# A second feed-forward net in two phases: gates and ups kept on chip, then the down product by seven block products

## The chip, the cores and the metric

The kernel runs on one core of a Trainium2 chip. Its engines run side by side, each through its own list of instructions in order: TensorE (PE; its weight loads are listed as PEld), VectorE (DVE), ScalarE (ACT), GpSimd (POOL) and SyncE (SP), which issues most transfers between the chip's main memory and the on-chip memory. Matmul results go to a second on-chip memory of eight banks, called PSUM in the code, from which VectorE and ScalarE read them. The metric is the time of one execution in microseconds of device time. Runs are repeated, and one execution is profiled.

## The reference, cut to what matters

Two layers of a diffusion backbone over 512 latent tokens and 256 context tokens, each with 1024 features. Layer 0 mixes tokens by gated linear attention and softmax attention, layer 1 by a gated recurrence; after each mixer stands a SwiGLU feed-forward net with a sandwich of norms and gates around it:

```python
def _swiglu(h, w_gate, w_up, w_down):
    return (jax.nn.silu(h @ w_gate) * (h @ w_up)) @ w_down
...
        x_lat = x_lat + m_lat[5] * _rms(_swiglu(h_lat, ffn_w_gate[l], ffn_w_up[l], ffn_w_down[l]), norm_post_ffn[l])
```

The hidden width is 2816, or 22 chunks of 128. In layer 1 only the 512 latent tokens go through the net. Everything is float32.

## The kernel before, in words

**Numbers.** Each float32 operand x of a large product is split into a high part H (a cast to the rounded format fp32r, on ScalarE) and a low part L = x - H (on VectorE). A product is then three matmuls, H H, H L and L H (`mm3`, line 679). Weights come in units of 128 x 1024 elements, 512 KB: one load into a `raw` tile (three buffers), one cast to `wH`, one subtraction to `wL` (four buffers each; `unit`, line 664).

**Gates and ups.** `h @ w_gate` and `h @ w_up` for a pair of chunks are made from block products after Strassen and Winograd: tokens, features and chunks are halved, and seven products of blocks take the place of eight (`SEVEN`, `seven`, line 768). `pair_operands` (line 730) loads two raw tiles and forms the sums of weight blocks on VectorE (line 752), which are split like the rest. A product of four feature blocks, three matmuls each, runs over n tokens; n is 256 in layer 1, 384 in layer 0. So a pair of chunks is 84 matmuls per weight. The banks are emptied by ScalarE and VectorE (lines 791 to 809) into a tile `go` for gates or `uo` for ups, one buffer each. The activation is applied in place at line 1572, the multiplication of ups by gates at line 1523.

**The loop of `ffn`** (line 1504) runs over the eleven pairs. The first pair, `first()`, is a plain product, begun while the norm before it still finishes. Then each turn makes a gate product, the part of the down product for the pair before (`acc_part`, line 811: 48 matmuls of 512 columns in layer 1, added to the result `y` by VectorE at line 820), and an up product. The gated pair is split at lines 1525 and 1526 into operands `gH` and `gL`, for which layer 1 reserves two sets (`forms.gated`). The last turn has no down part between; two down parts are then made together, and `post_norm` (line 644) closes each token tile: sum of squares, multiplication by the gate row, a power on GpSimd (line 600), and the last sum (line 659), which is stored.

**Order.** A scheduler behind the tile framework lays out each engine's list, by the order of the program and by readiness. Matmuls are pinned to program order only where `self.pinned` is set, which `ffn` does not do. Buffers of one tag are handed on when their readers are done; a pool opened where another was released waits for that pool's tiles one by one.

```python
        def gu(x):
            return fp.tile([P, 2, 2 * n], F32, tag=x, bufs=1, name=x)
...
            if c0 + 2 < NFC:
                if y is None:
                    y = yp.tile([P, len(tiles), D], F32, tag="y", bufs=1, name=f"y{l}")
                self.acc_part([(units(c0 - 2), cur)], n, tiles, singles, y, c0 == 2, fill)
                u = product(wu, c0, "uo")
```

Of the kernel before, what the change touches and what calls it, by code (L numbers as in the profile page):

```python
# [316 lines left out]
class Net:  # L317
# [29 lines left out]
    def mm(self, *a, **k):  # L347
        return self.pin(self.nc.tensor.matmul(*a, **k))  # L348
# [330 lines left out]
    def mm3(self, out, stat, mov, first, last):  # L679

        mm = self.mm
        mm(out, stat[0], mov[0], start=first, stop=False)
        mm(out, stat[0], mov[1], start=False, stop=False)
        mm(out, stat[1], mov[0], start=False, stop=last)

    def gemm_T(self, pt, W, h, groups, o=0):

# [77 lines left out]
            "U2": quarter(c, 0), "S4": quarter(c, 1), "V": quarter(d, 0),  # L765
        }

    def seven(self, W, h, X, fill, then=None):

        nc, n = self.nc, h.n  # L770
        ab = self.mm_tile("ab")
        bank = {"A": ab[:, :n], "B": ab[:, 512 : 512 + n]}
        c11, c12, c21, c22 = (X[:, i, n * k : n * k + n] for i in range(2) for k in range(2))
        for wn, hn, x in SEVEN:
            new = wn in ("11", "U1", "12", "22")
            if x not in bank:
                bank[x] = self.sc_tile(x, "ED".index(x))[:, :n]
# [12 lines left out]
            if wn == "11":  # L790
                nc.scalar.copy(c11, pt)  # L791
            elif wn == "U1":
                copy = nc.scalar.copy(c22, pt)
                if then is not None:
                    with self.tc.issue_after(copy.ins):
                        then()
                fill()
            elif wn == "12":
                nc.vector.tensor_tensor(c11, c11, pt, op=ALU.add)
            elif wn == "U2":  # L800
                nc.scalar.copy(c12, pt)
            elif wn == "22":
                nc.scalar.mul(c21, pt, -1.0)
                fill()
            elif wn == "S4":
                nc.vector.tensor_tensor(c12, c12, pt, op=ALU.add)  # L806
            else:
                nc.vector.tensor_tensor(c21, c21, pt, op=ALU.subtract)  # L808
                nc.vector.scalar_tensor_tensor(c22, pt, -1.0, c22, op0=ALU.mult, op1=ALU.subtract)  # L809
# [694 lines left out]
    def ffn(self, l, xp, yp, fp, pp, rp, h, ending, extra=None):  # L1504
# [95 lines left out]
        next(follow, None)  # L1600
        if gp is rp:
            rp.release()
        return y

    def run(self):
# [204 lines left out]

        def ending(ys):
            ep = self.open_pool("e1b")
            end = ender(ep, 1, 5, lat, xat(x1), lambda t: out[0, t * P : (t + 1) * P, :], None)

            def close():
                yield
                yield
                yield
                yield
                ep.release()  # L1820

            return end, close(), ep

        self.ffn(1, ha, yp, fp, pp, rp, forms, ending)
        fp.release()
        yp.release()
        ha.release()
        pad.release()


# [47 lines left out]
```

## Time and profile before

| what | value |
|---|---|
| runs, median of 3 | 1744.47 us (1738.44 to 1744.97) |
| profiled execution, its own time | 1732.31 us |
| span of the profiled execution, first to last instruction | 1730.5 us |
| mean granted TensorE clock | 0.999 |
| gates, ups and down product of layer 1, from the end of the first pair to the last matmul | 1391.7 to 1722.85 us |
| transfers, mean over the span | 108 GB/s |

A row of a group view names the line, the engine, the operation, the tile written and the tiles read, the shape and the count; then the busy time in microseconds, the mean of one in nanoseconds, and after the second bar the idle time of the engine just before these instructions, with what ended most of it. A row of the chain of waits gives a start, a length and the instructions that the end of the program goes back to. A row of windows gives a stretch of time and the busy microseconds of each engine in it, with the granted clock, the busy share of the transfer engines and their GB/s. A row of a timeline gives start, length, engine and instruction. A row of transfers gives the tile, the queue, the count, the size and the time from issue to landing. A row of waits gives who waited for whom: the sum in microseconds, the count, and the longest.

### The profile page before, as it was taken

To read this page: it belongs to the slowest core of one execution; us is meant where nothing else is said; L and a number is where in the kernel's file an instruction comes from. 1 tells how busy PE (TensorE), PEld (TensorE's weight loads), DVE (VectorE), ACT (ScalarE), POOL (GpSimd) and SP (SyncE) were. 2 spreads that over 40 slices of the span, in tenths; PEclk is the share of its full clock that TensorE was granted. 3 is DMA by queue.
4 is the path that set the end of the run, shared out by engine and by line. 5 is a ranking of instruction groups with operands and counts; after the bars stand their busy time and mean duration, and the time that the engine had idled before them with its cause. 6 is when DMAs were issued, how large, how long until landed. Compare 5 with 4: busy or idle time off the path is not lost. (4 is left out here: it accounts for less than half of the span.)

```text
span 1730.5 us, 32414 instructions
## 1 busy us (share of the span) xinstructions
PE 1681.9 (97%) x13512; PEld 1506.6 (87%) x13512; DVE 1288.3 (74%) x2061; ACT 863.7 (50%) x1496; POOL 73.3 (4%) x93
## 2 busy tenths in 40 slices
PE   7999998999999999999999999999999999999998
PEld 5899987888998889898997888889888899999997
DVE  5889668836969999796668328787864678878785
ACT  4745568746442323233346436666644754444342
POOL 1004110000000000000001000000000000000000
PEclk9999999999999999999999999999999999999999
DMA  9641012144334465452225222121114333333333
GB/s 321 195 143 39 2 62 88 61 134 146 111 97 144 133 193 171 131 179 62 74 86 186 82 73 62 42 59 51 50 62 141 116 110 99 94 102 110 94 102 122
DMA packets 169838, 187.22 MB, mean 108 GB/s; under 512 B 6454, under 2 KB 141148, under 8 KB 169692
## 3 DMA queue, kind: packets, MB, share of 16 engines
q1 hardware_dynamic: 167760, 181.56, 33.1%
q10 hardware_dynamic: 1932, 3.59, 0.6%
q8 instruction: 106, 1.74, 0.4%
q14 instruction: 40, 0.33, 0.1%
HBM read 175.66 MB, written 9.46 MB: 107 GB/s over the span
## 5 line engine op out<-in xcount | busy, mean ns | idle before, releaser
L348 PE MATMUL nat<-wH,x 128*128 128x256 f32 (+2 forms) x944 | 216.2, 319 | 5.1 <-ACT x L641 2.6
L673 DVE TENSOR_TENSOR wL<-raw,wH 128x1024 fp32r<-128x1024 f32 (+1 forms) x126 | 151.0, 1207 | 91.8 <-ACT wH L672 91.3
L727 ACT CAST wH<-raw 128x1024 fp32r<-128x1024 f32 x120 | 124.6, 1052 | 175.7 <-PE acc L348 73.6
L728 DVE TENSOR_TENSOR wL<-raw,wH 128x1024 fp32r<-128x1024 f32 x120 | 145.3, 1221 | 62.3 <-ACT wH L727 62.2
L348 PEld LDWEIGHTS nat<-wH,x 128*128 128x128 f32 x944 | 157.6, 190 | 21.5 <-ACT x L641 3.6
L348 PE MATMUL acc<-wH,gH 128*128 128x512 f32 x440 | 172.6, 393 | 0.0
L672 ACT CAST wH<-raw 128x1024 fp32r<-128x1024 f32 (+1 forms) x126 | 129.0, 1040 | 85.9 <-PE nat L348 25.2
L348 PE MATMUL acc<-wH,gL 128*128 128x512 f32 x440 | 171.7, 390 | 0.0
L348 PE MATMUL acc<-wL,gH 128*128 128x512 f32 x440 | 171.6, 390 | 0.0
L348 PE MATMUL nat<-wL,x 128*128 128x256 f32 (+2 forms) x472 | 148.6, 315 | 0.0
L820 DVE TENSOR_TENSOR y<-y,acc 128x1024 f32<-128x1024 f32 x135 | 114.9, 863 | 32.2 <-PE acc L348 28.8
L348 PE MATMUL ff<-x,wH 128*128 128x512 f32 (+1 forms) x512 | 127.5, 340 | 0.0
L530 DVE SCALAR_TENSOR_TENSOR macc<-mraw,scT,macc 128x1024 f32<-128x1024 f32 x98 | 123.0, 1281 | 5.0 <-DMA mraw<-in_mod_w_dram 4.7
L600 POOL TENSOR_TENSOR rs<-ms,neghalf 128x1 f32<-128x1 f32 (+2 forms) x62 | 57.2, 924 | 1582.6 <-DVE ms L598 1582.5
L348 PE MATMUL oproj<-wH,x 128*128 128x512 f32 x320 | 101.6, 395 | 0.0
L348 PEld LDWEIGHTS acc<-wH,gH 128*128 128x128 f32 x440 | 82.6, 188 | 19.7 <-issue 1.7
L348 PEld LDWEIGHTS acc<-wH,gL 128*128 128x128 f32 x440 | 82.6, 188 | 17.3
L348 PEld LDWEIGHTS acc<-wL,gH 128*128 128x128 f32 x440 | 82.7, 188 | 16.1
L348 PEld LDWEIGHTS ff<-x,wH 128*128 128x128 f32 x512 | 87.4, 190 | 10.0
L348 PEld LDWEIGHTS nat<-wL,x 128*128 128x128 f32 x472 | 89.8, 190 | 5.1
L923 ACT COPY qkh<-arr 128x512 f32<-128x512 f32 x112 | 70.1, 642 | 36.3 <-DVE arr L928 32.1
L348 PE MATMUL ff<-x,wL 128*128 128x256 f32 (+1 forms) x256 | 86.1, 337 | 0.0
(344 smaller groups left out, 4045.5 us busy)
## 6 DMA issues: line engine op xcount, KB each, us to landing
mraw<-in_mod_w_dram SPq DMA_DIRECT2D x80, 512.0 KB, 3.8
raw<-in_ffn_w_gate_dram SPq DMA_DIRECT2D x44, 512.0 KB, 3.7
raw<-in_ffn_w_up_dram SPq DMA_DIRECT2D x44, 512.0 KB, 4.0
raw<-in_ffn_w_down_dram SPq DMA_DIRECT2D x44, 512.0 KB, 3.5
raw<-in_odd_w_in_dram SPq DMA_DIRECT2D x40, 512.0 KB, 3.8
mraw<-in_mod_w_dram SPq DMA_DIRECT2D x32, 256.0 KB, 6.1
raw<-in_even_w_in_dram SPq DMA_DIRECT2D x16, 512.0 KB, 3.7
x<-xr SPq DMA_DIRECT2D x14, 512.0 KB, 2.6
```

What stands on the lines that cost most here:

```text
L348: return self.pin(self.nc.tensor.matmul(*a, **k))
L530: nc.vector.scalar_tensor_tensor(a, u, w, a, op0=ALU.mult, op1=ALU.add)
L600: nc.gpsimd.tensor_tensor(rs, ms, self.neghalf.to_broadcast([P, w]), op=ALU.pow)
L672: nc.scalar.copy(H[:, :m], raw[:, :m])
L673: nc.vector.tensor_tensor(L[:, :m], raw[:, :m], H[:, :m].bitcast(F32), op=ALU.subtract)
L727: self.nc.scalar.copy(H, f)
L728: self.nc.vector.tensor_tensor(L, f, H.bitcast(F32), op=ALU.subtract)
L820: nc.vector.tensor_tensor(y, y, pt, op=ALU.add)
L923: nc.scalar.copy(qkv[:, :, :, half, :], dst)
```

## The change

Layer 1's net gets a function of its own, `ffn_whole`; layer 0 keeps `ffn`. All gated products stay on chip as float32 in a tile `G`, 11 pairs x 2 x 512 tokens, so that the loop holds gate and up products alone. Gates alternate between `go` and a tile `other` laid where `y` will be; up products use the two `tr` banks for E and D (`turned`). In layer 0, `go` gets two buffers. The two reserved sets of gated operands are gone.

Then `down` makes the whole down product from seven block products. Tokens are halved (256 each), the 1024 output features are halved (512 each), and the 22 chunks are divided into even and odd ones, 11 each. The blocks of `G` are added and subtracted in place by VectorE (`sums`). The weight sums are not made by an engine: a tile `t` is loaded, used, and then a further block is added to it by a transfer with `accum_op` that GpSimd issues; so too `t3`. The weight is thus read several times. Each product runs in seven groups of one or two chunks (1, 1, 2, 2, 2, 2, 1). Product 0 reads its first four groups through `raw` tiles, since `t` lies where operands of the first phase lay, and loads them into `t` later. Operands of three groups at a time are kept ready, each with an `a` tile out of a ring of three. Two banks per set alternate between products (`X`, `O`); the matmuls are pinned to program order. The second half of the tokens is closed in product 4; of the last tile one half of the features is prepared in product 5 and the other closed at the end (`final`). The space reserved for descriptors of transfers that GpSimd issues is set to 2048 bytes.

```diff
-            return fp.tile([P, 2, 2 * n], F32, tag=x, bufs=1, name=x)
+            return fp.tile([P, 2, 2 * n], F32, tag=x, bufs=2 if x == "go" else 1, name=x)
...
+    def ffn_whole(self, l, xp, yp, fp, pp, rp, h, ending):
...
+        tp = first()
+        other = yp.tile([P, 2, 2 * n], F32, tag="y", bufs=1, name="go2")
...
+        for idx in range(1, np_):
+            c0 = 2 * idx
+            g = other if idx % 2 else go()
+            self.seven(self.pair_operands(tp, wg, c0 * P, [tp], 2), h, g, nothing, todo)
+            for k in range(2):
+                x = g[:, :, n * k : n * k + n]
+                nc.scalar.activation(x, x, AF.Silu)
+            x = G[:, idx]
+            self.seven(self.pair_operands(tp, wu, c0 * P, [tp], 2), h, x, nothing, None, True)
+
+            def todo(g=g, x=x):
+                for k in range(2):
+                    nc.vector.tensor_tensor(x[:, k], x[:, k], g[:, k], op=ALU.mult)
...
+        tp.release()
+        rp.release()
+        xp.release()
+        dp = self.open_pool(f"d{l}")
...
+    def down(self, dp, wd, G, y, tiles, n, ending):
...
+        groups = [slice(0, 1), slice(1, 2)] + [slice(i, min(i + 2, np_)) for i in range(2, np_, 2)]
+        near = 4
+        ring = lambda x: dp.tile([P, 2, n], F32R, tag=f"a{x}", bufs=3, name=f"a{x}")
...
+        add = lambda o, src: nc.gpsimd.dma_start(out=o, in_=src, accum_op=ALU.add)
+        load = lambda o, src: nc.sync.dma_start(out=o, in_=src)
+
+        def sums(p, i):
+            if p == 1:
+                v.tensor_tensor(A[1, 0][:, i], A[1, 0][:, i], A[1, 1][:, i], op=ALU.subtract)
+            elif p == 2:
+                v.tensor_tensor(A[0, 0][:, i], A[1, 0][:, i], A[0, 0][:, i], op=ALU.subtract)
+            elif p == 4:
+                v.scalar_tensor_tensor(A[1, 1][:, i], A[1, 1][:, i], -1.0, A[0, 0][:, i], op0=ALU.mult, op1=ALU.subtract)
+            elif p == 5:
+                v.tensor_tensor(A[0, 0][:, i], A[0, 0][:, i], A[0, 1][:, i], op=ALU.add)
...
+        def operands(p, g):
...
+            if p == 2:
+                load(t3[:, i], B(0, 1, i))
...
+            if p == 0 and g >= near:
+                load(t[:, i], B(0, 0, i))
+            if p >= 5 or p == 0 and g < near:
...
+                load(src, B(0 if p == 0 else 1, (0, 1, 0)[(0, 5, 6).index(p)], i))
+            else:
+                src = (t3 if p == 4 else t)[:, i]
+            sums(p, i)
...
+            nc.scalar.copy(H, src)
+            nc.scalar.copy(a[0], left[p][:, i])
+            v.tensor_tensor(L, src, H.bitcast(F32), op=ALU.subtract)
+            v.tensor_tensor(a[1], left[p][:, i], a[0].bitcast(F32), op=ALU.subtract)
+            if p == 0:
+                for x in ([g] if g >= near else []) + ([g - near] if g >= near else []) + ([near - 1] if g == len(groups) - 1 else []):
+                    j = groups[x]
+                    if x < near:
+                        load(t[:, j], B(0, 0, j))
+                    add(t[:, j], B(0, 1, j))
+            elif p < 3:
+                add(t[:, i], B(*more[p], i))
+            elif p == 3:
+                add(t3[:, i], B(1, 1, i))
...
+                    elif p == 4:
+                        v.tensor_tensor(y[:, t1, high], y[:, t1, high], out[i], op=ALU.subtract)
+                        v.tensor_tensor(y[:, t1, low], y[:, t1, low], out[i], op=ALU.add)
+                        end(y[:, t1, :], tiles[t1])
+                    elif p == 5:
+                        v.tensor_tensor(y[:, t0, high], y[:, t0, high], out[i], op=ALU.add)
+                        if i == nh - 1:
+                            close = final(dp, y[:, t0, :], tiles[t0])
...
-            if l:
-                forms.gated = [forms.gated_tiles(rp, k) for k in range(2)]
...
-                to = [[fp.tile([P, D], F32R, tag=x, bufs=1, name=f"o{x}") for x in ("go", "uo")]]
+                to = [[fp.tile([P, D], F32R, tag=x, bufs=2 if x == "go" else 1, name=f"o{x}") for x in ("go", "uo")]]
...
-    nc = bacc.Bacc("TRN2", target_bir_lowering=False, num_devices=1)
+    nc = bacc.Bacc("TRN2", target_bir_lowering=False, num_devices=1, dynamic_dma_scratch_size=2048)
```

More of the change, by code (lines that the diff above doesn't have):

```diff
@@ L766, in pair_operands, with seven @@
         }
-    def seven(self, W, h, X, fill, then=None):
+    def seven(self, W, h, X, fill, then=None, turned=False):
         nc, n = self.nc, h.n
@@ L1602, in ffn, with go, first @@
             rp.release()
+        return y
+    def ffn_whole(self, l, xp, yp, fp, pp, rp, h, ending):
+        nc, I = self.nc, self.I
+        wg, wu, wd = I["ffn_w_gate"][l], I["ffn_w_up"][l], I["ffn_w_down"][l]
+        tiles, n = h.order, h.n
+        np_, nh = NFC // 2, n // P
+        G = fp.tile([P, np_, 2, 2 * n], F32, tag="G", name="G")
+        def go():
+            return fp.tile([P, 2, 2 * n], F32, tag="go", name="go")
+        def first():
+            g = go()
+            us = [[self.unit_cols(w, i * P) for w in (wg, wu)] for i in range(2)]
+            h.open(xp)
+            for half in range(2):
+                pm = self.mm_tile("pearly")
+                pts = [[self.sc_tile("pearly", x)[:, :n] for x in range(2)], [pm[:, 512 * x : 512 * x + n] for x in range(2)]]
+                tok = slice(n * half, n * half + n)
+                for ks in ((range(4), range(4, 8)) if half == 0 else (range(8),)):
+                    for i in range(2):
+                        for m in range(2):
+                            for k in ks:
+                                self.mm3(pts[i][m], tuple(x[:, k, :] for x in us[i][m]), h.raw(k, half), k == 0, k == KD - 1)
+                            if ks[0] == 0 and half == 0 and m == 0:
+                                self.turn(1 - i)
+                for i in range(2):
+                    nc.scalar.activation(g[:, i, tok], pts[i][0], AF.Silu)
+                    nc.vector.tensor_tensor(G[:, 0, i, tok], g[:, i, tok], pts[i][1], op=ALU.mult)
+                if half == 0:
+                    pp.release()
+                    tp = self.open_pool(f"t{l}")
+                    h.sums(tp)
+            h.late()
+            return tp
+        tp = first()
+        other = yp.tile([P, 2, 2 * n], F32, tag="y", bufs=1, name="go2")
+        nothing = lambda: None
+        todo = None
+        for idx in range(1, np_):
[10 more added lines that the diff above has]
+                    nc.vector.tensor_tensor(x[:, k], x[:, k], g[:, k], op=ALU.mult)
+        todo()
+        tp.release()
+        rp.release()
+        xp.release()
+        dp = self.open_pool(f"d{l}")
+        y = self.down(dp, wd, G, yp.tile([P, len(tiles), D], F32, tag="y", bufs=1, name=f"y{l}"), tiles, n, ending)
+        return y
```

140 lines of the change are left out of this document (125 added, 15 removed).

## The prediction

> **What bounds the kernel now.** I read the page's busy lines first, then its transfer queues.
>
> ```profile
> span 1730.5 us, 32414 instructions
> PE 1681.9 (97%) x13512; PEld 1506.6 (87%) x13512; DVE 1288.3 (74%) x2061; ACT 863.7 (50%) x1496; POOL 73.3 (4%) x93
> ...
> q1 hardware_dynamic: 167760, 181.56, 33.1%
> q10 hardware_dynamic: 1932, 3.59, 0.6%
> q8 instruction: 106, 1.74, 0.4%
> q14 instruction: 40, 0.33, 0.1%
> ```
>
> TensorE is busy 97% of the span, so this change pays through fewer matmuls. The two data queues belong to SP and ScalarE. None belongs to GpSimd, so an adding transfer is nowhere in this trace. Next come the windows of the stage to be replaced, one turn of its loop (a gate product, the down product of the pair before, an up product), and a window of layer 0's feed-forward net.
>
> ```profile
> 1458.70:1490.80 32.10, 31.29 (x216) 29.21 (x216) 25.69 (x37) 14.01 (x22) 0.00 (x0) 1.00 0.34 100
> ...
> 600.00:700.00 100.00, 98.20 (x516) 89.29 (x516) 92.73 (x114) 36.85 (x51) 0.00 (x0) 1.00 0.55 174
> ```
>
> Columns: TensorE, weight loads, VectorE, ScalarE, GpSimd, granted clock, transfer share, GB/s. TensorE is full, the clock whole, transfers a third used, VectorE 80%. In layer 0 VectorE runs at 93% and TensorE still at 98%, so a crowded VectorE need not cost time. The chain that ended last gives the price of matmuls; the groups of TensorE from 1360 us on give the counts.
>
> ```profile
> 1590.51 1.44 PE ab L348 x12
> ...
> 1594.95 10.92 PE acc L348 x48
> ...
> 1627.02 10.92 PE acc L348 x48
> ```
>
> ```profile
> L348 PE MATMUL acc<-wH,gH 128*128 128x512 f32 x176 | 68.6, 390 | 0.0
> L348 PE MATMUL acc<-wL,gH 128*128 128x512 f32 x176 | 68.6, 390 | 0.0
> L348 PE MATMUL acc<-wH,gL 128*128 128x512 f32 x176 | 68.5, 389 | 0.0
> ```
>
> The 390 ns are a pipelined duration. The chain gives the pace: 10.92/48 = 227.5 ns for 512 columns, 1.44/12 = 120 ns for 256. A block product of 84 matmuls takes 10.08 us, a down part 10.92. A turn needs 2 x 10.08 + 10.92 = 31.1 us and lasts 32.1 (from 1594.95 to 1627.02). The whole stage after its first pair needs 20 x 10.08 + 528 x 0.2275 = 321.7 us. It runs from 1391.7 to the last matmul, 1722.85, or 331.1 us: 9.4 us are idle. The waits of TensorE name half of them (first two rows from 1364 us on, the third in layer 0).
>
> ```profile
> PE ab L348 <- ACT go L791: 4.0, 8, 1.0
> ...
> PE ab L348 <- DVE uo L799: 0.7, 1, 0.7
> ```
>
> ```profile
> PE ab L348 <- ACT go L791: 1.9, 2, 1.4
> ```
>
> L791 copies into the single gate tile, which it may overwrite only after L1523 has multiplied with it.
>
> **The change part by part.** (1) Matmuls. A product of the down phase is 2 token tiles x 11 chunks x 3 = 66 matmuls of 512 columns, the seven are 462 instead of 176 x 3 = 528. 66 x 0.2275 = **-15.0 us**.
>
> (2) Idle time. With two gate tiles and no down part between products, the 4.7 us named above go. Of the other 4.7 I give up a quarter: **-6 us**; bounds -9.4 (all) and -3 (new hand-overs of the same size).
>
> (3) Phase one must feed a block product every 10.08 us, where now there are two in 32.1. The rows are VectorE's and ScalarE's by shape from 1400 us on.
>
> ```profile
> L728 DVE TENSOR_TENSOR wL<-raw,wH 128x1024 fp32r<-128x1024 f32 x57 | 68.9, 1221 | 29.1 <-ACT wH L727 29.0
> L752 DVE TENSOR_TENSOR raw<-raw 128x512 f32<-128x512 f32 x57 | 39.2, 687 | 0.7
> L820 DVE TENSOR_TENSOR y<-y,acc 128x512 f32<-128x512 f32 x36 | 24.7, 686 | 7.0 <-PE acc L348 5.3
> ...
> L809 DVE SCALAR_TENSOR_TENSOR go<-ab,go 128x256 f32<-128x256 f32 x10 | 4.2, 419 | 0.0
> ...
> L659 DVE SCALAR_TENSOR_TENSOR xr<-pn,rs,xr 128x1024 f32<-128x1024 f32 x3 | 3.9, 1286 | 0.9 <-POOL rs L600 0.7
> L652 DVE TENSOR_TENSOR pn<-y,gv 128x1024 f32<-128x1024 f32 x3 | 3.7, 1223 | 0.1
> ```
>
> ```profile
> L727 ACT CAST wH<-raw 128x1024 fp32r<-128x1024 f32 x57 | 59.0, 1049 | 50.2 <-PE acc L348 33.3 <-PE ab L348 6.6 <-DMA raw<-in_ffn_w_up_dram 6.3
> ...
> L727 ACT CAST dH<-ws 128x512 fp32r<-128x512 f32 x19 | 11.8, 620 | 37.5 <-PE acc L348 23.9 <-DVE ws L752 13.6
> ```
>
> VectorE per block product: three splits of 1024 (3.66), one of 512 (0.69), four sums of 512 (2.75), four evictions of 256 (1.68), one gating multiply of 512 (0.69), 9.5 us of 10.08. That is as full as layer 0's window, which kept TensorE at 98%. The three raw buffers must turn over too. The page's transfer rows give the landing.
>
> ```profile
> raw<-in_ffn_w_gate_dram SPq DMA_DIRECT2D x44, 512.0 KB, 3.7
> raw<-in_ffn_w_up_dram SPq DMA_DIRECT2D x44, 512.0 KB, 4.0
> ```
>
> The second raw tile of a product can take the place of the last product's second: 4.0 to land, two sums (1.4), a cast (1.05), a split (1.22), a sum (0.69), 8.4 us, under 10.08. Cost **0**, hidden under TensorE with 1.7 us to spare; if the turn-over fails, see rival three. The raw loads queue on SP, in order, with nothing else behind them but the next product's.
>
> (4) Entry of the down phase. Operand ring, t and t3 lie where the old operands of the products lay. The ring lies on the tile that the third of the seven products reads last, so it is free 5.8 us early; t and t3 wait for the last one, which is why the first four groups use raw. **+1 us** (0 to 3).
>
> (5) The adding transfers, unknown here. A block of the down weight is 11 chunks x 256 KB = 2.88 MB. Rates of a saturated stretch, from the start of the program:
>
> ```profile
> 0.00:43.00 43.00, 30.35 (x351) 24.82 (x351) 21.47 (x58) 20.64 (x38) 5.01 (x15) 1.00 0.98 323
> ...
> 2.00:12.00 10.00, 3.27 (x13) 2.50 (x13) 3.99 (x10) 6.60 (x14) 2.90 (x4) 1.00 0.99 378
> ```
>
> Between 323 and 378 I take 350 GB/s: 8.2 us a block. Product 0 lasts 66 x 0.2275 = 15.0 us. Product 1 needs its fourth group, the last to be added, after 15 chunks of 6 x 0.2275 = 1.365 us, 20.5 us, less 2.5 us for cast and split: landed by 18 us. Until then t (8.2) and its add (8.2 if an add costs what a load does) fit, 16.4. But t3 waits for nothing SP has not waited for already, so its 8.2 us compete: 24.7, **+6.7 us late**. The bounds are 0 (t3 goes behind) and 15 (t3 in front and adds at twice a load's price, 8.2 + 16.5 + 8.2 = 32.9). Double price without t3 in front gives 6.7 again, hence my value. Later products must add 2.88 MB in 15.0 us, 192 GB/s, and hide at single or double price. GpSimd's queue takes 28 adds, in order; the first waits for the split of group 4, and behind them stand the small powers of the norms (next row, L600), for which VectorE waits. All adds are issued by product 3, the first norm comes in product 4. Of an issue only this is near:
>
> ```profile
> L600 POOL TENSOR_TENSOR rs<-ms,neghalf 128x1 f32<-128x1 f32 (+2 forms) x62 | 57.2, 924 | 1582.6 <-DVE ms L598 1582.5
> ```
>
> Seven issues at 0.9 us per 15.0 us hide; twice that would too. SP issues 32 loads for the down weight where it issued 22, without waits on TensorE but for t, t3 and the raw buffers. The smaller descriptor space has no row; I take 0, inside these bounds.
>
> (6) VectorE in the down phase. Per chunk: a half split of 1024 (0.61), of 512 (0.35), a sum (0.35), 1.30 us against 1.365. In products 4 and 5 come six evictions of 512 (4.1), two norms (2 x 2.5) and half a norm's product (0.7): 22 x 1.30 + 9.8 = 38.4 against 30.0. Of 8.4 too much the three groups of lookahead (two ahead are 5.5 us) hide some: **+5 us** (0 to 8). ScalarE needs a half cast of 1024 and of 512, 0.83 us per chunk, and hides.
>
> (7) Tail. TensorE's last matmul and VectorE's timeline:
>
> ```profile
> 1722.46 0.39 PE L348 MATMUL acc<-wH,gL 128*128 128x512 f32 x1
> ```
>
> ```profile
> 1721.53 0.69 DVE L820 TENSOR_TENSOR y<-y,acc 128x512 f32<-128x512 f32 x1 [1.37 <-PE acc L348]
> 1722.13 1.29 DVE L659 SCALAR_TENSOR_TENSOR xr<-pn,rs,xr 128x1024 f32<-128x1024 f32 x1
> 1723.34 0.68 DVE L820 TENSOR_TENSOR y<-y,acc 128x512 f32<-128x512 f32 x1
> ```
>
> The last add of y waits 0.5 us behind another tile's norm, and then two halves are multiplied by the gate where one will be left (0.69): **-1.2 us** (-2 to 0).
>
> (8) The second gate tile in layer 0 takes away at most the 1.9 us of the row above: **-1 us** (-2 to +2, other orders).
>
> Sum: -15.0 - 6 + 0 + 1 + 6.7 + 5 - 1.2 - 1 = **-10.5 us**. The profiled execution took 1732.3 us, 1.8 around its span, and would take 1721.8. It lies 12.2 us under the median of the runs, 1744.5, so the forecast for a median is **1734 us**. Ends of all terms: -15 - 9.4 - 2 - 2 = -28 (1716), and -15 - 3 + 3 + 15 + 8 + 2 = +10 (1754).
>
> **Rivals.** *One: an add costs twice a load.* It would read the old sum as well as the weights. Then the wait at product 1 is 15 us and not 6.7: -2 us, 1742, no change. Nothing in the trace speaks against it; for it, that a packet must move two operands. The Trainium skill, "Collectives: The Full Stack", section on why ReduceScatter is half of AllGather, has this rule for adds between cores: the add itself is free, the second read halves the rate. No run here shows it yet; by that rule this rival would be the case.
>
> *Two, slower: the adds set the pace.* If adds run under 192 GB/s, products 1 to 3 each wait for theirs. At three times a load's price a block takes 24.7 us: 8.2 + 24.7 + 8.2 = 41 at product 1, 23 late (16 more than forecast), then 9.7 each in products 2 and 3: -10.5 + 16 + 19 = +25, 1769. Place: first matmuls of products 1, 2 and 4, waiting for a cast behind a GpSimd transfer. Against it: the transfer share is 0.34 here.
>
> *Three, slower: phase one is paced by the raw buffers.* If a product's second raw tile gets the buffer that comes free last, two more sums or casts and a split enter the circle: 8.4 + 0.7 + 1.05 + 1.22 = 11.3 us. 20 x 1.2 = 24 us, +14, 1758. It decides from 10.08 us on. For it: the chain that ended last already passes through up-weight loads; against it: the free 1.7 us.
>
> *Four: no gain in (2)*, because the idle time was hand-over between products: 1737; inside the forecast.
>
> **How the numbers follow.** Forecast 0.55, rival one 0.20, two 0.13, three 0.12. Half a per cent, 8.7 us, is about what a measurement of this kernel tells from no change. Faster: 0.47 of the forecast's 0.55 and a quarter of rival one's 0.20, together 0.52. Same: 0.08 and 0.10 of these, 0.03 of rivals two and three, 0.21. Slower 0.27. The forecast's own range is 1716 to 1754; with the slow rivals' nearer half the range becomes 1717 to 1764.
>
> **What would show it.** Down matmuls 462, at 227 ns. Phase one: block products 10.1 to 10.2 us apart; at 11 or more rival three holds. The first matmul of product 1 should start 15 to 17 us after that of product 0 and its fourth group some 7 us late, with casts waiting for a GpSimd transfer; packets of that queue at twice 2 KB's time speak for rival one, at three times for two. TensorE should wait about 5 us in product 5 for splits. The forecast is wrong if the waits before products 1 to 3 exceed 20 us in all.

## The result, and the profile after

The changed kernel takes 1756.30 us (median of five runs, 1755.54 to 1757.16); the kernel before, run beside it, takes 1738.44. The ratio is 1.0098, with a 95% interval of 1.0081 to 1.0115: slower by 1%, where 1734 and faster was forecast. The time lies inside the stated range, 1717 to 1764, on the side of its slow rivals. The profiled execution took 1757.16 us, 24.9 more than the profiled one of before, which lay some 6 us under its own median.

The page of the changed kernel, busy times and the two large transfer queues:

```profile
span 1755.4 us, 32537 instructions
...
PE 1677.8 (96%) x13446; PEld 1500.4 (85%) x13446; DVE 1299.3 (74%) x2099; ACT 895.5 (51%) x1550; POOL 104.1 (6%) x121
...
q1 hardware_dynamic: 171504, 183.13, 33.5%
q0 software_dynamic: 6080, 11.54, 3.6%
```

The 66 matmuls are gone, and TensorE's busy time fell by only 4 us. New is q0, GpSimd's queue: packets, MB, and the time that they took as a share of sixteen engines' span. 3.6% of 1755.4 us is 63 us of all the engines for 11.54 MB, or 183 GB/s.

Windows of the changed kernel, from the end of the first pair to the last matmul; the columns are the engines' busy times as before, then the granted clock, the transfer share and GB/s. The bounds are phase one, products 0 to 3, products 4 and 5, product 6, cut where the first matmul of each begins:

```profile
1395.40:1604.70 209.30, 205.55 (x1682) 202.65 (x1680) 174.89 (x261) 112.43 (x183) 0.00 (x0) 1.00 0.35 102
1604.70:1695.40 90.70, 66.75 (x265) 53.21 (x265) 54.10 (x84) 38.09 (x62) 30.20 (x28) 0.87 0.95 216
1695.40:1731.50 36.10, 31.60 (x133) 24.37 (x132) 28.76 (x41) 19.86 (x33) 1.42 (x2) 1.00 0.46 153
1731.50:1748.00 16.50, 15.71 (x67) 12.05 (x66) 12.58 (x16) 8.48 (x14) 0.55 (x1) 1.00 0.27 81
```

The second row is the result. Four products of 15.0 us last 90.7, with the transfer engines at 0.95, VectorE busy for 0.60 of the stretch and ScalarE for 0.42. What TensorE waited for in the whole down phase, from 1600 to 1750 us:

```profile
PE whole L348 <- ACT y L1792: 13.6, 1, 13.6
PE whole L348 <- DVE y L1796: 5.9, 1, 5.9
PE whole L348 <- DVE aL L1727: 4.1, 2, 2.4
PE whole L348 <- DVE y L1801: 1.4, 1, 1.4
PE whole L348 <- DVE y L1804: 1.3, 1, 1.3
PE whole L348 <- ACT y L1794: 1.0, 1, 1.0
PE whole L348 <- ACT y L1798: 1.0, 1, 1.0
PE whole L348 <- DVE y L1808: 0.8, 1, 0.8
```

Most releasers named are the copies `y` that empty the banks at a product's end. The timeline of ScalarE shows what stood in front of the first one:

```profile
1622.76 0.41 ACT L1725 CAST aH<-G 128x256 fp32r<-128x256 f32 x1 [1.04 <-PE whole L348]
1635.65 1.04 ACT L1724 CAST wH<-tb 128x1024 fp32r<-128x1024 f32 x1 [12.48 <-DMA tb<-in_ffn_w_down_dram]
1636.60 0.58 ACT L1792 COPY y<-whole 128x512 f32<-128x512 f32 x1
```

A copy that was ready near 1623 began at 1636.6, behind a cast of the next product, and ScalarE had waited 12.5 us for that cast's adding transfer. The granted clock fell too: after the waits of 2.4, 13.6 and 5.9 us it went down to 0.50 and was back after 3 to 5 us, and after those of 1.0 to 1.7 us it stayed at 1.00. So the 264 matmuls of the four products kept TensorE busy for 66.75 us, where 60.1 are needed at the full pace. Three candidates were open: the price of the adding transfers, their order, and the copies.

### The profile page after: what moved, and what is told of

It reads as the page before. It is cut to its first block, busy times and chain, and to the rows that moved or that the text cites. A ratio compares the mean times of both kernels' runs of the same rounds, so it can differ in the third digit from the quotient of the medians.

```text
span 1755.4 us, 32537 instructions
## 1 busy us (share of the span) xinstructions
PE 1677.8 (96%) x13446; PEld 1500.4 (85%) x13446; DVE 1299.3 (74%) x2099; ACT 895.5 (51%) x1550; POOL 104.1 (6%) x121
## 3 DMA queue, kind: packets, MB, share of 16 engines
q0 software_dynamic: 6080, 11.54, 3.6%
## 4 chain that ended last, share of the span: by engine, by line
PE 68%; DVE 12%; DMA 8%; ACT 5%; issue 4%; POOL 2%; DVEq 0%; SPq 0%; POOLq 0%; ACTq 0%
PE nat L348 11%; PE ab L348 10%; PE ff L348 8%; PE acc L348 8%; PE oproj L348 5%; PE E L348 5%; DMA raw<-in_ffn_w_up_dram 4%; PE pearly L348 2%; PE fq L348 2%; PE D L348 2%; PE whole L348 2%; PE gqk L348 2%; DVE wL L728 2%; DMA mraw<-in_mod_w_dram 2%; PE S L348 1%
## 5 line engine op out<-in xcount | busy, mean ns | idle before, releaser
L673 DVE TENSOR_TENSOR wL<-raw,wH 128x1024 fp32r<-128x1024 f32 (+1 forms) x104 | 124.2, 1203 | 83.7 <-ACT wH L672 83.0
L348 PEld LDWEIGHTS nat<-wH,x 128*128 128x128 f32 x944 | 157.7, 190 | 21.6 <-ACT x L641 3.6
L672 ACT CAST wH<-raw 128x1024 fp32r<-128x1024 f32 (+1 forms) x104 | 106.7, 1038 | 80.1 <-PE nat L348 25.1
L348 PE MATMUL acc<-wH,gH 128*128 128x512 f32 x264 | 104.1, 395 | 0.0
L348 PE MATMUL acc<-wH,gL 128*128 128x512 f32 x264 | 103.2, 391 | 0.0
L348 PE MATMUL acc<-wL,gH 128*128 128x512 f32 x264 | 103.0, 390 | 0.0
L348 PEld LDWEIGHTS ff<-x,wH 128*128 128x128 f32 x512 | 87.4, 190 | 10.1
L348 PE MATMUL whole<-wH,aH 128*128 128x512 f32 x154 | 63.3, 411 | 24.9 <-ACT y L1792 13.6
L752 DVE TENSOR_TENSOR raw<-raw 128x512 f32<-128x512 f32 x120 | 82.5, 688 | 2.2
L820 DVE TENSOR_TENSOR y<-y,acc 128x512 f32<-128x512 f32 (+1 forms) x81 | 68.8, 860 | 19.3 <-PE acc L348 17.7
L348 PE MATMUL ab<-T,wH 128*128 128x384 f32 (+1 forms) x320 | 73.4, 319 | 7.6 <-DVE G L799 3.5
```

Of the source, the lines that this page charges most:

```text
L672: nc.scalar.copy(H[:, :m], raw[:, :m])
L673: nc.vector.tensor_tensor(L[:, :m], raw[:, :m], H[:, :m].bitcast(F32), op=ALU.subtract)
L752: add = lambda o, x, y: nc.vector.tensor_tensor(o, x, y, op=ALU.add)
L820: nc.vector.tensor_tensor(y, y, pt, op=ALU.add)
```

## The experiments

All ratios are to the kernel before, run beside each kernel on the same chip.

**1. The second gate tiles alone**, in the kernel before (`bufs=2 if x == "go" else 1` at both places and the small descriptor space).

> The kernel before with two gate tiles alone (in both feed-forward nets; the smaller descriptor space makes room for the second tile in layer 0, and no transfer of GpSimd is in this kernel). If the idle time named by the waits for L791 was the single gate tile's (4.0 us in layer 1, 1.9 in layer 0), it is 4 to 6 us faster than before, ratio 0.997. If that wait only hides another hand-over, it is within 1 us, ratio 1.000.

Measured: 1733.05 us, 0.9970 (0.9959 to 0.9981). The 4.0 us of waits for `go` at L791 are gone from its trace; 2.7 us of waits for L799 came in their place. This part of the change is a gain of some 5 us.

**2. The second sum's loads held back**: an element of each group of `t3` is written after product 1's split, so that the load must follow it.

```diff
             v.tensor_tensor(a[1], left[p][:, i], a[0].bitcast(F32), op=ALU.subtract)
+            if p == 1:
+                v.tensor_copy(t3[:, i, 0:1], L.bitcast(F32)[:, :, 0:1])
```

> The changed kernel with the loads of t3 held back: each waits for the low part of its group in product 1, through a one-column copy on VectorE. Theory A (an adding packet takes 178 ns against 84 of a plain one, and t3's loads, which alternate with it packet by packet, push it from 203 to 131 GB/s): the add of 2.88 MB for product 1 takes 14.2 us and not 22, so the wait before product 1 falls from 13.6 to about 6 us; t3 then competes in products 1 and 2, and the waits there grow by up to 7; in all 0 to 8 us faster than the changed kernel. Theory B (GpSimd issues too slowly, or has no room for descriptors): the wait before product 1 stays at 13 to 14 us.

Measured: 1754.04 us, 1.0093 (1.0079 to 1.0107). The wait at product 1 went from 13.6 to 12.9 us only, and products 0 to 3 took 88.8 us in place of 90.7. Theory A had the wait fall to 6 us; that `t3` competes early is a small part.

**3. The same transfers without the addition.** This leaves out the weight sums: each addition becomes a plain load of the same block into the same place.

```diff
-        add = lambda o, src: nc.gpsimd.dma_start(out=o, in_=src, accum_op=ALU.add)
+        add = lambda o, src: nc.gpsimd.dma_start(out=o, in_=src)
```

> The changed kernel with GpSimd's adding transfers replaced by plain loads of the same bytes on the same queue (the weight sums are left out, so the weight blocks used are not the sums). Theory A: a packet takes 84 ns, a block 8 us, and the waits for transfers before products 1 and 3 fall from 19.5 to under 5 us, with the slow clock behind them: 15 to 22 us faster than the changed kernel, about 1736 to 1741. Theory B: the issue times and gaps on GpSimd stay, the wait before product 1 stays above 10 us, and the kernel gains under 8 us.

Measured: 1739.97 us, 1.0008 (0.9996 to 1.0020), 16 us less than the changed kernel. GpSimd's queue on its page, and its products 0 to 3:

```profile
q0 software_dynamic: 3264, 11.54, 1.8%
```

```profile
1603.60:1679.50 75.90, 63.74 (x265) 50.94 (x265) 55.04 (x85) 37.71 (x62) 18.22 (x28) 0.96 0.71 259
```

The same 11.54 MB take 1.8% of 1739.4 us, 31 us or 369 GB/s, in 3264 packets. So an addition costs twice a load: 63 us against 31, and 6080 packets. This is rival one's price. The Trainium skill, "Collectives: The Full Stack", section "The bandwidth ceiling", says of adds between cores that the second read halves the rate; the trace agrees with the half for adds into on-chip memory, 183 against 369 GB/s; that the second read is the reason is shown by no run here.

The addition is not the whole loss: the four products still take 75.9 us. TensorE waits 6.6 us at the end of product 0, which is what part (5) of the prediction had at a load's price, and 1.1 at the end of product 2.

**4. Twice the descriptor space**, 4096 bytes; GpSimd's issues in the changed kernel stand up to 3.7 us apart with nothing shown that they wait for.

> The changed kernel with twice the descriptor space (4096 bytes). Theory B in its form that GpSimd waits for room (gaps of 2.8 to 3.7 us ahead of adds that no wait explains, 29.6 us in all): the gaps shrink, adds start 3 to 10 us earlier, and the kernel is 3 to 10 us faster. Theory A: the gaps shrink, but the transfer engines are full either way and the time stays within 1.5 us.

Measured: 1754.40 us, 1.0089 (1.0074 to 1.0104). The unexplained gaps fell from 29.6 to 0.2 us in all, and the time by 2, just outside theory A's 1.5 and short of theory B's 3. GpSimd then waited elsewhere for the same transfers.

**5. The copies after both halves.** The last three matmuls of a product's second half of tokens wait for the copy of the first half, since both lie in one tile of two banks. Here the copies come after both.

```diff
-                if g == len(groups) - 1:
+                for i in [] if g < len(groups) - 1 else [i] if p == 6 else range(nh) if i == nh - 1 else []:
```

> The changed kernel with one edit: the two copies of a product's sums out of PSUM come after the last three matmuls of its second half of the tokens, not between the halves. Theory A (the wait of about 1 us at each product's end is one of the product with itself: both halves lie in one PSUM tile, so the last three matmuls of the second half wait for the copy of the first, and before products 1 and 3 that copy stands behind a cast that waits for an adding transfer): five waits of 1.0 to 1.4 us go, 5 us in all, and products 1 and 3 begin with the two groups that are ready, 2.7 us each, before they wait; the transfers then still set the pace of products 0 to 3, so only part of it comes through: 1747 to 1752 us, and what is left of the two long waits stands on the casts' operands (wH, wL or aL) and no longer on the copies y. Rival B (the wait is the time in which the copy frees the banks for the next product): the waits stay, 1755 to 1757 us.

Measured: 1756.46 us, 1.0105 (1.0086 to 1.0123). What TensorE waited for in the down phase:

```profile
PE whole L348 <- ACT aH L1725: 17.8, 4, 10.7
PE whole L348 <- DVE aL L1727: 7.1, 3, 3.9
PE whole L348 <- DVE y L1808: 0.8, 1, 0.8
PE whole L348 <- DVE wL L1726: 0.5, 2, 0.2
```

The cause of the small waits was read rightly: every wait for a copy is gone but the last. The gain was not. Products 0 to 3 took 89.5 us (90.7 before this edit), products 4 and 5 took 36.9 (36.1). The waits only moved to the operands. In each of the two stretches something else set the pace.

**6. The sums on GpSimd's arithmetic**, with plain loads.

```diff
-        add = lambda o, src: nc.gpsimd.dma_start(out=o, in_=src, accum_op=ALU.add)
+        def add(o, src):
+            s = dp.tile([P, 2, 512], F32, tag="s", bufs=3, name="s")[:, : o.shape[1]]
+            nc.sync.dma_start(out=s, in_=src)
+            nc.gpsimd.tensor_tensor(o, o, s, op=ALU.add)
```

> The changed kernel with its weight sums made by GpSimd's arithmetic: each adding transfer becomes a plain load by SP into one of three new buffers and an addition of 128x512 or 128x1024 numbers on GpSimd, by its one like row (128x512 in 1.19 us) some 13 us of each 15 us product. Theory A (the loss is the transfers' price: products 0 to 3 need 11.5 MB of adds at about 200 GB/s and some 7 MB of loads, 76 us for 60 us of matmuls): at plain price the transfers take 48 us, so the time falls by 10 to 16 us, to 1740 to 1747 us, and the DMA share falls below 1 after product 2. Rival B (the loss is the chain load, add, cast, which any adder has): the wait before product 1 stays at 10 us or more, 1752 to 1760 us. Rival C (GpSimd's additions are slower, or slow VectorE): VectorE's split of 128x1024 takes clearly over 1.22 us, or GpSimd is busy throughout and the products come 17 us or more apart; 1755 us or more.

Measured: 1762.81 us, 1.0141 (1.0120 to 1.0161); rival C. VectorE's and GpSimd's groups in the down phase:

```profile
L1730 DVE TENSOR_TENSOR wL<-tb,wH 128x1024 fp32r<-128x1024 f32 x14 | 32.8, 2347 | 1.7 <-ACT wH L1728 1.7
...
L1730 DVE TENSOR_TENSOR wL<-raw,wH 128x1024 fp32r<-128x1024 f32 x9 | 11.0, 1220 | 0.0
```

```profile
L1691 POOL TENSOR_TENSOR tb<-tb,s 128x1024 f32<-128x1024 f32 x12 | 33.2, 2769 | 11.1 <-DVE wL L1730 9.9 <-DMA s<-in_ffn_w_down_dram 1.1
```

The split of 128x1024 takes 2.35 us where GpSimd adds and 1.22 where it doesn't, in one run. VectorE became the bound: 97.4 us busy of 99.3 in products 0 to 3. The Trainium skill, "SBUF — State Buffer", section "SBUF: two separate sides", has a reason: VectorE, reading two operands, and GpSimd take one pair of ports by turns, each for a whole instruction. The trace fits it, with 1.13 us of delay for each split as its number.

**7. Experiment 6 with the edits of 2 and 5, and another order**: product 1 asks for the first four groups first, and their sums now go ahead of the others.

```diff
-                for x in ([g] if g >= near else []) + ([g - near] if g >= near else []) + ([near - 1] if g == len(groups) - 1 else []):
+                for x in () if g < near else (0, 1) if g == near else (2, near) if g == near + 1 else (3, near + 1, near + 2):
```

> All at once, as a version that might beat both kernels: sums on GpSimd with plain loads, copies after both halves, the sums of the first four groups made ahead of the others (product 1 asks for them first), and the second sum's loads held back until product 1 splits. Theory A (transfer price, then order, then the copies): products 15.2 to 16 us apart, no wait over 3 us, 1727 to 1735 us against 1738 of the kernel before. Rival B (GpSimd's additions set the pace): 1738 to 1750 us with waits for tb on ACT from the second product on.

Measured: 1767.07 us, 1.0169 (1.0140 to 1.0197), slower than either range. Rival B's sign, casts that wait for `tb`, is absent (0.3 us); VectorE's split took 1.91 us there, and TensorE waited for the splits. So VectorE beside GpSimd sets the pace here too.

**8. That order with the adding transfers**: experiment 7 without the edit of 6.

> As the last one, but with the adding transfers kept: copies after both halves, adds of the first four groups ahead of the others, second sum's loads held back. Theory A (the engines of the transfers are full from the first product to the fourth, so order only moves the wait): the wait before product 1 falls from 13.6 to under 6 us and waits come up in products 2 to 4; over products 0 to 3 still some 80 us; 1742 to 1750 us. Rival B (order and the copies are the whole loss): products 15.5 us apart throughout, 1730 to 1738 us.

Measured: 1754.18 us, 1.0091 (1.0074 to 1.0109). The total missed theory A's range by 4 us, and products 0 to 3 took 87.4 us where some 80 were expected. The mechanism held: the wait at product 1 fell to 5.3 us, waits of 2.9 and 4.2 came up later, and the transfer share is 0.99.

```profile
1602.40:1689.80 87.40, 71.82 (x265) 55.01 (x265) 51.66 (x87) 37.25 (x60) 30.26 (x28) 0.88 0.99 224
```

So order moves the wait, and the four products last as long as their transfers.

**9. The sums made earlier, in main memory.** GpSimd's queue writes the four sums to main memory during phase one, a copy and then an adding transfer for each group, and the products load each block plainly through a ring of six buffers. `t` and `t3` are gone.

```diff
+        S = [self.dr.tile([P, np_, 512], F32, name=f"sum{x}") for x in range(4)]
...
+                nc.gpsimd.dma_start(out=S[o][:, i], in_=S[a][:, i] if type(a) is int else B(*a, i))
...
+                nc.gpsimd.dma_start(out=S[o][:, i], in_=B(*b, i), accum_op=ALU.add)
...
+            load(src, B(0, 0, i) if p == 0 else B(1, 6 - p, i) if p >= 5 else S[p - 1][:, i])
```

> The changed kernel with its weight sums moved in time: GpSimd's queue makes the four sums in DRAM during phase one (a copy and an adding transfer for each group, 11.5 MB of either; the DMA engines are 0.3 to 0.4 busy there and GpSimd has nothing else to do), and the block products load each block plainly through a ring of six buffers. The arithmetic of every other engine is that of the changed kernel. Theory A (the loss of products 0 to 3 is the adding transfers' time on the DMA engines, 76 of the 90 us that they take): products 0 to 3 take 64 to 68 us in place of 90, products 4 and 5 stay at 35 to 37, which VectorE sets, and phase one grows by 0 to 6 us: 1730 to 1740 us. Rival B (not the transfers: casts, splits and copies of the down phase set its pace): products 0 to 3 still take 80 us or more, 1748 us or more. Rival C (phase one pays for it, its raw loads come late beside the sums): phase one is over 10 us longer and the gain is given back, 1742 to 1757 us.

Measured: 1800.03 us, 1.0348 (1.0329 to 1.0366). Phase one went rival C's way, far beyond its range of 1742 to 1757, and the down phase theory A's, 1.6 us above its 64 to 68. Windows: phase one, products 0 to 3, products 4 and 5:

```profile
1396.40:1670.10 273.70, 217.59 (x1683) 214.16 (x1681) 175.37 (x261) 111.89 (x183) 38.20 (x47) 0.90 0.60 153
1670.10:1739.70 69.60, 62.99 (x265) 50.42 (x265) 55.08 (x85) 37.28 (x61) 0.00 (x0) 0.98 0.64 205
1739.70:1775.10 35.40, 31.68 (x134) 24.43 (x133) 28.64 (x41) 20.38 (x34) 1.42 (x2) 1.00 0.61 203
```

Products 0 to 3 fell from 90.7 to 69.6 us, while VectorE and ScalarE had the same work (55.1 and 37.3 us busy, 54.1 and 38.1 in the changed kernel). Phase one grew from 209.3 to 273.7.

**10. Experiment 9 with the edit of 5:**

> The last one, with the copies of a product's sums after both halves. Theory A (the wait of 1.0 to 1.4 us at each product's end was hidden in the fifth experiment only because the transfers, and VectorE in products 4 and 5, set the pace anyway): now products 0 to 3 are free of the transfers and gain 3 to 4 us, products 4 and 5 gain nothing: 2.5 to 5 us less than the last one, 1726 to 1736 us. Rival B (VectorE sets the pace throughout): within 1.5 us of the last one.

Measured: 1794.60 us, 1.0315 (1.0295 to 1.0336), 5.4 less. Products 0 to 3 took 64.7 us in place of 69.6, and products 4 and 5 went from 35.4 to 36.7:

```profile
1670.80:1735.50 64.70, 62.22 (x266) 50.67 (x266) 52.77 (x83) 36.79 (x60) 0.00 (x0) 0.97 0.69 221
```

So the edit that gave nothing in experiment 5 is worth 5 us where the transfers don't set the pace, and nothing in products 4 and 5.

**11. Experiment 10 with the sums paced**: eight parts, each released by the gated pair before.

> The tenth kernel with its sums spread over phase one: three copies and three adding transfers for each of eight pairs of block products, held back until the gate-up product of the pair before is there (24 of each in all, the same bytes). In the tenth run the same transfers filled the DMA engines for 105 us and phase one grew by some 62 us, while the down phase shrank to 118 us. Theory A (phase one lost there because the engines were full at once; the sums need some 90 us of the engines and phase one leaves some 130 of its 206 free): phase one 204 to 216 us, down phase 117 to 120 us, 1731 to 1744 us. Rival B (any adding transfer that stands beside the raw loads makes them late, full engines or not, since three raw buffers cover only 5 us of landing): phase one over 225 us, 1752 us or more.

Measured: 1753.76 us, 1.0097 (1.0080 to 1.0114), rival B's time. Phase one took 231.5 us, 22 more than in the changed kernel, with the transfer share at 0.72:

```profile
1395.80:1627.30 231.50, 209.79 (x1682) 205.97 (x1681) 175.03 (x261) 112.33 (x183) 39.87 (x49) 0.99 0.72 183
```

Landing times of the raw gate weights from 1400 to 1600 us, and the busy tenths of the transfer engines in 40 slices of the same time, in the changed kernel and then here:

```profile
raw<-in_ffn_w_gate_dram SPq DMA_DIRECT2D x17, 512.0 KB, 4.8
DMA  4634337253333342515070705142434215140413
```

```profile
raw<-in_ffn_w_gate_dram SPq DMA_DIRECT2D x17, 512.0 KB, 12.0
DMA  7242489961699973999679994999759994799715
```

These loads are late: they land after 12.0 us in place of 4.8 (those of the other weight after 4.6, before 4.8), where phase one needs two loads every 10 us and has three buffers. VectorE waited 27.8 us for raw tiles in phase one, against 11.3 in the changed kernel, and TensorE 21.6 us in all, mostly for VectorE's work on the banks, against 3.5. The mean share hides bursts: each part is six transfers at once, and in 19 of the 40 slices the engines are nine tenths busy or more. So this run does not tell whether the loads are late only where the engines are full.

**12. The same parts still earlier**, one after each of the eight per-head norms of layer 1's mixer, 30 us apart, where raw loads come 9 us apart. A small transfer of the norm's result into the sum's tile holds each part back.

```diff
                     rs = self.rstd(ss, P, LT)
+                    self.down_sums(hd, rs)
```

> The eleventh kernel with the same sums made earlier: in eight parts of three copies and three adding transfers, one after each of the eight per-head norms on GpSimd between 1086 and 1308 us, which come 30 us apart; the DMA engines are 0.15 to 0.24 busy there, and the raw loads come 9 us apart (29 in 270 us). Theory A (phase one lost in the eleventh run because its raw loads, one each 5 us, come late beside adding transfers): here the loads have 9 us each, so the stretch grows by 0 to 8 us, phase one returns to 205 to 208 us and the down phase keeps 116 to 120 us: 1728 to 1740 us, below the changed kernel by 17 us or more. Rival B (loads and small transfers come late here too, and GpSimd's norms stand behind its transfers): the stretch from 1086 us to the first gate-up product grows by over 15 us, 1745 us or more.

Measured: 1737.58 us, 1.0004 (0.9995 to 1.0013), as theory A had it. What was left to lose lay at the mixer's end: TensorE 92.0 us busy from 1250 to 1350 us, against 97.2 in the changed kernel, and the eight raw loads of the output projection landed after 9.2 us in place of 4.3.

**13. The same sums in the first six heads.** What was open before this run was whether that loss is the last two parts beside the output projection's loads.

```diff
-        o, a, b = ((0, (0, 0), (0, 1)), (3, (0, 1), (1, 1)), (1, 0, (1, 1)), (2, 1, (1, 0)))[at // 2]
...
+        now = [(*c, i) for c in chain for i in pairs][4 * at : 4 * at + 4]
```

> The twelfth kernel with the same sums in the first six heads (four copies and four adding transfers in each, 1083 to 1260 us) and none beside the output projection's loads. Theory A (in the twelfth run the stretch from 1250 to 1350 us lost some 5 us, PE 92.0 busy against 97.2 in the changed kernel, because the last two parts made the projection's raw loads late): the stretch is back at 96.5 to 97.5 us busy and the total falls by 4 to 6 us, to 1731 to 1735 us, 0.2 to 0.4% below the kernel before. Rival B (the loss there is not the sums' or moves with them to the heads): within 2 us of the twelfth, 1735.5 us or more.

Measured: 1727.58 us, 0.9938 (0.9923 to 0.9954), faster than before by 0.6% and than experiment 1, whose interval lies above. It is 10.0 us under experiment 12 by medians and 6.7 by the spans of the profiles, where 4 to 6 were expected; what goes beyond the mixer's end is not explained. Windows: the heads, the mixer's end, products 0 to 3, products 4 and 5:

```profile
1083.00:1260.00 177.00, 177.00 (x2173) 156.72 (x2172) 142.54 (x315) 111.01 (x191) 63.13 (x78) 1.00 0.72 178
1250.00:1350.00 100.00, 97.53 (x787) 81.37 (x786) 55.53 (x97) 44.88 (x69) 7.88 (x10) 1.00 0.45 133
1600.80:1665.40 64.60, 62.11 (x265) 50.61 (x265) 52.58 (x82) 36.69 (x60) 0.00 (x0) 0.97 0.69 221
1665.40:1701.20 35.80, 32.17 (x133) 25.83 (x133) 29.23 (x42) 20.76 (x36) 1.95 (x2) 0.95 0.59 198
```

In the heads TensorE is busy without a break at a transfer share of 0.72, the very share that cost phase one 22 us; the engines are nine tenths busy or more in 20 of 36 slices of 5 us from 1083 us on, about as often as in experiment 11. One thing that differs is that the raw loads come one in some 9.6 us, not two in 10, and they land after 5.1 us. Why they land sooner is not shown. The mixer's end is back at 97.5 us busy, with the projection's loads landing after 4.6 us, and the four products have their 64.6 us. Against the changed kernel's span the profile has 30.6 us less, of which products 0 to 3 are 26.1.

## Why the prediction was wrong, point by point

The forecast's sum, -10.5, and the profiled difference, +24.9, are 35.4 us apart. The windows divide them.

**The step that failed is (5), the adding transfers**, and in it the sentence that later products "must add 2.88 MB in 15.0 us, 192 GB/s, and hide at single or double price". It allowed 6.7 us of wait in products 0 to 3, and with (4) 7.7 in all; they lost 90.7 - 60.1 = 30.6. That is 23 of the 35 us. Three things were wrong with it. It contradicts its own price: twice 8.2 is 16.5 us a block, as its own bound of 15 for product 1 counts it, and 16.5 us do not hide in 15.0. The price was double: by its packets' time an addition runs at 183 GB/s, under the 192 that rival two named as its edge. And the method: each block was timed against its own product, with one competitor, and the bytes were not summed over the stretch. The four blocks of additions take 63 us of the engines, and the loads of the same stretch what remains of 0.95 x 90.7 = 86 us, 23 us. 86 us don't go into 60, in whatever order, as experiments 2, 4 and 8 show, and with the sums elsewhere the four products take 64.6. So rival two happened, at rival one's price: the adds set the pace already at twice a load's price, not only at three times. Their combination had no line of its own.

What TensorE did divides the 23 us further. 6.9 are the wait at product 0's end, 13.6 for 6.7; here the forecast's chain of load and add was right, 6.6 at a load's price (experiment 3) and within its bound of 15 at twice that. 5.9 are the wait at product 2's end, where the adds were to hide. 6.7 are matmuls at a lower clock after the long waits, 2.0 are copies between the halves of products 1 and 3, and 1.4 are (4); for the clock and the copies the forecast had no term. Undone by experiments, in this order, the 30.6 us are 14.8 for the addition itself (experiment 3, 75.9 us), 6.3 for the transfers that experiment 9 takes out of the stretch besides (69.6), 4.9 for the copies (experiment 10, 64.7), and 4.6 that stay: 2.4 of (4) and the lower clock behind it. The prediction's own sign of failure, waits before products 1 to 3 of over 20 us in all, came true by little: 13.6 + 1.0 + 5.9 = 20.5.

The other 12.5 of the 35.4 us are, rounded, 4.3 in (2), 4.7 in (8), 1.5 in product 6, which took 16.5 us for 15.0, 1.1 in (6) and 1.0 in (7).

**(1)** 66 matmuls fewer, and the pace of full clock as before; right. Part of it was given back within the failed stretch, where the granted clock was 0.87.

**(2) and (3)** Phase one's products came 209.3/20 = 10.5 us apart, between the 10.1 to 10.2 forecast and rival three's 11. 209.3 - 201.6 = 7.7 us were idle where 9.4 - 6 = 3.4 were allowed: the gain is 1.7 us, under the lower bound of 3. TensorE's named waits of L791 are gone, as forecast; waits of 3.5 us for VectorE's additions from the banks (L799) came in their place, so the new hand-overs were larger than the bound had them. Rival four, no gain here, comes near; its 1737 is a slip, since the sum without (2) gives 1740. Experiment 1 had its 5 us from the same tiles with the old loop.

**(4)** The first matmul of the down phase follows the last block product at once; 2.4 us are lost two matmuls later, for a split. Forecast 1, within 0 to 3.

**(6)** Products 4 and 5 lost 36.1 - 30.0 = 6.1 us, forecast 5, and experiments 5, 9, 10 and 13 leave it at 5 to 7 whatever else they change. The mechanism is told rightly for product 5 only, and the size is in part luck. VectorE is busy 15.3 of the 16.2 us from 1709.9 to 1726.1, and a split comes 1.7 us late there, where 5 were forecast for splits. Over both products VectorE is busy 28.8 of 36.1 us and not 38.4, since it does sums for them ahead of their time, and the waits for copies, 1.4 and 1.3 us, come to more than the one for the split. With the copies moved (experiment 5) the split comes 3.9 us late instead, which fits that their order gives nothing in these two products.

**(7)** From the last matmul to the end 7.4 us, where 7.65 were; 0.25 gained of 1.2.

**(8)** could not be separated in the changed kernel: its first pair ends 3.7 us later than before, in part beside a drop of the clock (below). The prediction's 1391.7 for the kernel before is half a microsecond late: its first block product begins at 1391.2. By that mark (2) gained half a microsecond more, and (8) lost as much more.

**Not foreseen:** the copies between the two halves of a product, 1.0 to 1.4 us each. In this kernel they gain nothing when they are removed, since other things set the pace (experiment 5); freed of the transfers they are worth 5 us (experiment 10).

By medians the change cost 17.9 us where 10.5 of gain were forecast, 28.4 apart; the profiled pair shows 7 more, since the profiled execution of before lay 6 under its median. The time itself is missed by 22 us, because the forecast started from 1744.5, the median of three, where the later runs have 1738.4.

## What to carry to other kernels

Where transfers take over an engine's work, sum their engine time over the whole stretch that needs them, at the price of each kind, and compare it with the stretch; a check product by product hides a deficit that every order only moves. An edit that removes a true wait can give nothing while another resource sets the pace of that stretch, as the copies' order did here, and its full worth once that is gone, so test it again then. A mean share of the transfer engines under one does not show room: the same 0.72 cost 22 us where two loads were needed every 10 us, and nothing where one was. So move work to a free queue where the other loads are few, and look at their landing times.

## What the runs showed of the hardware

An adding transfer into on-chip memory costs two loads' time (183 against 369 GB/s for the same bytes). Beside copies and adding transfers into main memory, one of two streams of plain loads landed in 12.0 us in place of 4.8. GpSimd's addition of 128x1024 numbers takes 2.8 us, and VectorE's split of that size takes 2.35 us beside such additions in place of 1.22. And a short idle time can lower the clock or not: the same wait of 1.9 us, for a norm ahead of transposes, is followed by a mean clock of 0.66 in the changed kernel (first row, from the last 0.6 us of the wait on) and of 1.00 in the kernel before (second row, which holds the wait itself):

```profile
1376.00:1381.00 5.00, 4.36 (x25) 4.39 (x26) 4.22 (x6) 3.69 (x11) 0.00 (x0) 0.66 0.11 39
```

```profile
1372.00:1377.00 5.00, 3.07 (x27) 3.06 (x27) 3.62 (x6) 3.49 (x11) 0.55 (x1) 1.00 0.33 134
```

Why it dropped in the one and not in the other was not tried.
